# Attention scores on the whole array: key tiles with high and low parts in two halves of the rows

## The chip, the cores and the metric

The kernel runs on one core of one Trainium2 chip. The core has a matrix engine (TensorE, PE in the profile; PEld is its weight load), a vector engine (VectorE, DVE), an activation engine (ScalarE, ACT), a general engine (GpSimd, POOL) and an engine that only issues transfers (SyncE, SP). Each engine works through its own queue in order; semaphores tie the queues together. The on-chip memory has 128 partitions (rows); matrix results land in a separate memory, PSUM, in banks of 512 float32 per partition. The metric is the device time of one execution in microseconds (us); lower is better.

## The reference

Two layers act on a sequence of 1024 tokens of width 1024, in float32: first a gated linear recurrence, then sliding-window attention. Each is followed by a layer norm, a gated feed-forward part with a short convolution, and another layer norm. The change touches the attention alone:

```python
# 16 query heads, 4 key/value heads, head size 64, window 128; block j of 128 queries sees key blocks j-1 and j
q = (h @ w_q).reshape(B, nb, 128, 4, 4, 64)
logits = einsum('bntgrd,bnsgd->bngrts', q, keys_of_blocks_j_minus_1_and_j) * 64 ** -0.5
logits = where(mask, logits + bias, -inf)
m = maximum(logits.max(-1), sink)
p = exp(logits - m[..., None])
o = einsum('bngrts,bnsgd->bntgrd', p, values) / (p.sum(-1) + exp(sink - m))
mix = o.reshape(B, S, D) @ w_out
```

Keys and values are projected once, from the output of the first layer.

## The kernel before

**Float32 products.** TensorE multiplies in a rounded format (`F32R`). So most operands are kept as a high part (the rounded value, made by a ScalarE copy) and a low part (the value less its high part, made by a VectorE subtraction in `low_part`), and a product is three matmuls: high by high, high by low, low by high. These are lines L169 to L171 in `mm3`, with 512 or 256 columns. Plain float32 matmuls are L175 (`mm32`), transposes L179 (`tr`). `split`, `split_into` and `unit` make the two parts of a loaded weight in the buffer `HL` (ScalarE L151, VectorE L144) or of activations in `T`, the transposed input of all projections (ScalarE L196, VectorE L144).

**Start of the attention stage (L1097 to L1316).** While the second layer norm of layer 1 still finishes its last four token blocks (`ln_mid`: VectorE L232, transposes L179, ScalarE L244 and VectorE L246 out of one PSUM tile, then the split into `T`), `k_part` projects keys, `v_part` values, each for a part of the tokens. `k_part` gets, per half of 512 tokens and per pair `c` of key heads, one PSUM tile `ps` with head e = 0 in partitions 0 to 63 and head e = 1 in 64 to 127 (`es` is a head's own half of the partitions, `os` the other one). ScalarE writes the high part of each head into both halves of the partitions of `Kh` (L1133, L1134), VectorE the low part into `Kl` (L1136).

**Queries.** There are eight column groups c = 0..7, each one query head of two key groups (e = 0, 1; 128 columns). `q_proj` projects group c + 1 in two halves of 512 tokens while group c is attended. `q_split` then makes, out of the PSUM tile, the high part in the head's own partitions (ScalarE L1186, two instructions of 64x512) and the low part in the other partitions of the same tile `q` (VectorE L1188, two instructions).

**Scores.** `attend(c, bp, q)` is a generator that takes two blocks of 128 queries (bp = 0..3) through seven stages, with a `yield` after each: (1) scores on TensorE (L1200: queries' high and low rows by `Kh`, the whole array; L1203: the high rows of one head by `Kl`, half the rows) and ScalarE's copy of the scores of the block itself into `X` (L1205); (2) VectorE puts the scores of the block before over the masked places (L1209), GpSimd adds the bias (L1212, L1215); (3) VectorE takes the maximum (L1220, L1223), ScalarE the exponentials and their sums (L1227, L1229); (4) VectorE normalises (L1231 to L1233); (5) TensorE transposes (L179); (6) VectorE masks out of PSUM into `W` (L1241); (7) TensorE multiplies by the values (L175), ScalarE copies the result into `Y` (L1254) or, for c = 7, splits it into `T`.

**Order.** The loop from L1319 writes the order of TensorE, ScalarE, VectorE and GpSimd out by hand: what an engine gets in this loop it runs in just this order. A step (c, bp) runs stage 1 of its own blocks, stage 7 of the blocks three steps back, stage 3 of those one step back, stage 2 of its own, stages 5 and 6 of those two steps back, a quarter of the next group's projection (12 matmuls of `mm3`), stage 4 of those one step back, then `q_split` of a half that is done (at bp = 2 for half 0 and at bp = 0 of the next group for half 1), then the low parts that wait in the list `lows`. At bp = 0 of c < 6 ScalarE then casts the query weights of group c + 2 (L151); from c = 5, bp = 1 on, at the end of four steps, it casts parts of the output weights, and `Y_to_T` casts attention results into `T`. In the second step `v_part(3)` is put in between. Semaphores are placed by the framework from the reads and writes of each tile, not by hand.

PSUM tiles: `psmm` (one bank, four buffers) for projections, transposes and value products, `psax` (two banks, two buffers) for the scores.

Of the kernel before, what the change touches and what calls it, by code (L numbers as in the profile page):

```python
# [10 lines left out]
F32 = mybir.dt.float32  # L11
F32R = mybir.dt.float32r
U8 = mybir.dt.uint8
AF = mybir.ActivationFunctionType
ALU = mybir.AluOpType

P = 128
S = 1024
# [69 lines left out]
def trunk(ctx: ExitStack, tc: tile.TileContext, a: dict, out: bass.AP):  # L88
    nc = tc.nc
# [25 lines left out]
    def psmm():  # L115
        return mmp.tile([P, 512], F32, name="psmm")

    def psax():
        return axp.tile([P, 1024], F32, name="psax")
# [9 lines left out]
    def raw_tail(pool):  # L129
        tail["raw"] = [pool.tile([P, 1024], F32, name=f"raw{i}") for i in range(3)]  # L130
# [37 lines left out]
    def mm3(ps, st, mv, start, stop, n=512):  # L168
        nc.tensor.matmul(ps, st(0), mv(0), start=start, stop=False)  # L169
        nc.tensor.matmul(ps, st(0), mv(1), start=False, stop=False)  # L170
        nc.tensor.matmul(ps, st(1), mv(0), start=False, stop=stop)  # L171
        od.t += 3 * n / 2365.0
# [9 lines left out]
    def proj_T(hl, half, ps):  # L182
        for kc in range(KC):
            mm3(ps, lambda i: hl[:, i, kc, :], lambda i: T[:, i, kc, half * 512:(half + 1) * 512],
                kc == 0, kc == KC - 1)
            od.tick()
# [476 lines left out]
    with tc.tile_pool(name="t", bufs=1, reuse_waits="tile") as raws, hgrn_pool as hp:  # L663
# [40 lines left out]
        with tc.tile_pool(name="ep", bufs=1, reuse_waits="tile") as ep:  # L704
# [50 lines left out]
            ps = psmm()  # L755
# [212 lines left out]
        for i in range(2 * pairs):  # L968
            for s in range(8 * NH):
                for r in free:  # L970
                    at = next(n for n in range(s + 2, 9 * NH) if n not in busy and n not in sums)
# [99 lines left out]
        ps = psax()  # L1071
# [25 lines left out]
    with (tc.tile_pool(name="ta", bufs=1, reuse_waits="tile") as raws,  # L1097
          tc.tile_pool(name="at", bufs=1, reuse_waits="tile") as at):
        raw_tail(raws)
        Kh = at.tile([P, 2, 2, S], F32R, name="Kh")  # L1100
        tri = at.tile([P, 2, P], F32, name="tri")
        nc.scalar.dma_start(tri, a["tri"])
        sk = at.tile([P, 16], F32, name="sk")
# [7 lines left out]
                                                       ap=[[0, P], [1, 512]]))  # L1111
        wkv = a["shared_w_kv"]
        wkvv = wkv.rearrange("(kc p) c -> p kc c", p=P)
        Kl = at.tile([P, 2, S], F32R, name="Kl")
        Vt = at.tile([P, NB, 256], F32, name="Vt")
        khl, uv = [], []
        for c in range(2):
# [8 lines left out]
        def k_part(half):  # L1126
            ts = slice(half * 512, (half + 1) * 512)
            for c in range(2):
                ps = psmm()
                proj_T(khl[c], half, ps)  # L1130
                heads = [(slice(64 * e, 64 * e + 64), slice(64 - 64 * e, 128 - 64 * e)) for e in range(2)]
                for e, (es, os) in enumerate(heads):
                    nc.scalar.copy(Kh[es, c, e, ts], ps[es])  # L1133
                    nc.scalar.copy(Kh[os, c, e, ts], ps[es])  # L1134
                for e, (es, os) in enumerate(heads):
                    nc.vector.tensor_tensor(Kl[es, c, ts], ps[es], Kh[es, c, e, ts].bitcast(F32), op=ALU.subtract)  # L1136
        nsk = at.tile([P, 16], F32, name="nsk")
        nc.gpsimd.tensor_scalar(nsk, sk, -1.0, None, op0=ALU.mult)

# [27 lines left out]
        def q_proj(hl):  # L1167
            qs, done = [], []
            yield qs, done
            for half in range(2):  # L1170
                q = at.tile([P, 2, 512], F32R, name="q", bufs=3)
                qs.append(q)
                ps = psmm()
                for kc in range(KC):
                    mm3(ps, lambda i: hl[:, i, kc, :], lambda i: T[:, i, kc, half * 512:(half + 1) * 512],
                        kc == 0, kc == KC - 1)
                    od.tick()
                    if kc % 2 == 1 and kc < KC - 1:
                        yield
                done.append((q, ps))  # L1180
                yield

        def q_split(q, ps):
            heads = [(slice(64 * e, 64 * e + 64), slice(64 - 64 * e, 128 - 64 * e)) for e in range(2)]
            for e, (es, os) in enumerate(heads):
                nc.scalar.activation(q[es, e, :], ps[es], AF.Copy, scale=0.125)  # L1186
            for e, (es, os) in enumerate(heads):
                nc.vector.scalar_tensor_tensor(q[os, e, :], ps[es], 0.125, q[es, e, :].bitcast(F32),  # L1188
                                               op0=ALU.mult, op1=ALU.subtract)

        def attend(c, bp, q):
            pp, r = divmod(c, 4)
            ps = psax()
            pv = ps.rearrange("p (e j s) -> p e j s", e=2, j=2)
            for jj in range(2):
                j = 2 * bp + jj
                lo = P if j == 0 else 0
                qs, ks = slice((j % 4) * P, (j % 4 + 1) * P), slice((j - 1) * P + lo, (j + 1) * P)
                for e in range(2):
                    nc.tensor.matmul(pv[:, e, jj, lo:], q[bp // 2][:, e, qs], Kh[:, pp, e, ks], start=True, stop=False)  # L1200
                for e in range(2):
                    es = slice(64 * e, 64 * e + 64)
                    nc.tensor.matmul(pv[:, e, jj, lo:], q[bp // 2][es, e, qs], Kl[es, pp, ks], start=False, stop=True)  # L1203
            X = at.tile([P, 2, 2, P], F32, name="X", bufs=4)
            nc.scalar.copy(X, pv[:, :, :, P:])  # L1205
            yield
# [48 lines left out]
            else:  # L1255
                ts = slice(bp * 256, (bp + 1) * 256)
# [36 lines left out]
        with tc.manual_schedule(engines={EN.PE, EN.Activation, EN.DVE, EN.Pool}):  # L1293
            od.finish(lns[:4])
            late = [od.spawn(ln_rows(range(1), rows, 2.5, h2d), 6.0)]
            k_part(0)
            for tp in range(3):
                od.finish(lns[2 * tp:2 * tp + 2])
# [4 lines left out]
            hl = q_unit(0)  # L1303
            make_lows()
            k_part(1)
            g = q_proj(hl)
            q, done = next(g)
            hl = q_unit(1)
# [10 lines left out]
            for c in range(8):  # L1319
                fill = q_proj(hl) if c < 7 else last_filler()  # L1320
                nq, nd = next(fill)
                for bp in range(4):
                    it = attend(c, bp, q)
                    prev = [None] * (3 - len(flight)) + flight
                    if 4 * c + bp in moves:
                        Y_to_T(*moves[4 * c + bp], lows)
                    stage(it)
                    stage(prev[0])
                    stage(prev[2])
                    stage(it)  # L1330
                    stage(prev[1])
                    stage(prev[1])
                    stage(fill)
                    stage(prev[2])
                    while done:
                        q_split(*done.pop(0))
                    make_lows()
                    if bp == 0 and c < 6:
                        hl = q_unit(c + 2)
                    stage(fill)  # L1340
                    if len(flight) > 2:
                        flight.pop(0)
                    done.extend(nd)
                    nd.clear()
                    if c == 0 and bp == 1:
                        v_part(3)
                    if 0 <= 4 * c + bp - 21 < 4:
                        ring["hl"] = 4 * c + bp - 21
                        us.extend(out_unit(rows2, 4 * c + bp - 21, lows))
                    flight.append(it)  # L1350
                q = nq
            a29, a30, a31 = flight
            for _ in range(2):
                ps = psax()
# [55 lines left out]
```

## Time and profile before

| what | value |
|---|---|
| median of three runs | 2218.3 us (2216.71 to 2218.33) |
| span of the profiled execution, first to last instruction | 2212.6 us |
| TensorE busy | 2177.4 us (98%) |
| VectorE busy | 1787.0 us (81%) |
| ScalarE busy | 931.6 us (42%) |
| GpSimd busy | 177.7 us (8%) |
| steps of the attention loop | from 1291.7 to about 1476 us of the span |

The profiled execution's own time is its span; the rest up to the median of the runs lies before its first and behind its last instruction. Times in the rows count from the span's start. A row of the view in order of time has start, length, engine, line, operation, output <- inputs, shape, and how many equal instructions in a row it merges; in square brackets stands the idle time before it and what ended that. The ends of matmuls are modelled, so the distance between two starts tells more than a length. A row of waits has the waiting instruction, what it waited for, the total time, how often and the longest. A row of groups has the count, total busy time, mean time of one in ns, and the idle time before.

### The profile page before, as it was taken

Reading aid. Unit: us, or ns where it says so; the run is one execution under the profiler, and the core shown is the slowest. Engines: PE = TensorE matmul, PEld = TensorE weight load, DVE = VectorE, ACT = ScalarE, POOL = GpSimd, SP = SyncE. Lnnn points to the kernel's source line nnn. Section 1 sums busy time; section 2 is a strip of 40 time slices with the busy share of each in tenths; the row PEclk is TensorE's granted clock in tenths of the full one; section 3 lists DMA queues with packets and bytes.
Section 4 is the critical chain, followed back from the end, with each engine's and each line's share of the span. In section 5 each row is a group of like instructions: output and inputs, shape, how many; then the busy total and the mean of one; then the engine's idle time right before and its main releaser. Section 6 shows DMA issues by size and latency. Waiting matters only on the chain.

```text
span 2212.6 us, 33398 instructions
## 1 busy us (share of the span) xinstructions
PE 2177.4 (98%) x13135; PEld 1812.6 (82%) x13135; DVE 1787.0 (81%) x2415; ACT 931.6 (42%) x1601; POOL 177.7 (8%) x196
## 2 busy tenths in 40 slices
PE   8999999999999999999999999999999999999998
PEld 7888888888888888887888887778888888887887
DVE  2777666566789888888997788887899888889987
ACT  4333333332844443344334446655554443343431
POOL 0121111210100000000000012211000000000001
PEclk9999999999999999999999999999999999999999
DMA  5555443252222222238854431114123222249663
GB/s 196 191 191 172 153 172 116 69 125 86 87 85 86 84 78 86 86 96 272 279 171 130 115 89 34 34 63 138 67 96 96 78 75 85 86 144 318 202 215 134
DMA packets 231943, 281.16 MB, mean 127 GB/s; under 512 B 29977, under 2 KB 160746, under 8 KB 228970
## 3 DMA queue, kind: packets, MB, share of 16 engines
q1 hardware_dynamic: 228736, 276.53, 38.5%
q10 hardware_dynamic: 3050, 2.49, 0.9%
q8 instruction: 103, 1.69, 0.3%
q14 instruction: 54, 0.44, 0.1%
HBM read 213.96 MB, written 65.01 MB: 126 GB/s over the span
## 4 chain that ended last, share of the span: by engine, by line
PE 82%; DVE 9%; DMA 3%; ACT 3%; issue 2%; POOL 1%; SPq 0%; ACTq 0%; DVEq 0%; POOLq 0%
PE psmm L169 17%; PE psmm L171 16%; PE psmm L170 16%; PE psax L171 8%; PE psax L169 8%; PE psax L170 8%; PE psax L175 3%; DVE T L144 1%; PE psmm L175 1%; DMA rx<-in_ffn_w_in_dram 1%; DVE HL L144 1%; PE psax L179 1%; ACT Y L244 1%; PE psax L1200 1%; PE psax L1203 1%
## 5 line engine op out<-in xcount | busy, mean ns | idle before, releaser
L169 PE MATMUL psmm<-T,HL 128*128 128x512 f32 x768 | 308.1, 401 | 0.0
L170 PE MATMUL psmm<-T,HL 128*128 128x512 f32 x768 | 300.7, 392 | 3.8 <-DVE T L144 2.1
L171 PE MATMUL psmm<-T,HL 128*128 128x512 f32 x768 | 301.3, 392 | 0.0
L474 DVE SCALAR_TENSOR_TENSOR Y<-Y,cwt 128x1023 f32<-128x1023 f32 (+1 forms) x176 | 225.3, 1280 | 40.1 <-ACT Y L472 39.9
L472 ACT ACTIVATE Y<-Y,cwt 128x1024 f32<-128x1024 f32 x88 | 109.1, 1240 | 263.6 <-DVE Y L461 260.0
L169 PE MATMUL psmm<-HL,T 128*128 128x256 f32 (+1 forms) x656 | 199.6, 304 | 1.5 <-ACT T L196 1.5
L171 PE MATMUL psmm<-HL,T 128*128 128x256 f32 (+1 forms) x656 | 195.4, 298 | 1.6 <-DVE T L144 1.6
L170 PE MATMUL psmm<-HL,T 128*128 128x256 f32 (+1 forms) x656 | 195.1, 297 | 1.2 <-DVE HL L144 1.2
L196 ACT CAST HL<-rx 128x1024 fp32r<-128x1024 f32 (+1 forms) x137 | 140.3, 1045 | 122.6 <-DMA rx<-in_ffn_w_in_dram 33.3
L144 DVE TENSOR_TENSOR HL<-rx,HL 128x1024 fp32r<-128x1024 f32 (+1 forms) x137 | 165.9, 1213 | 14.9 <-ACT HL L196 14.3
L171 PEld LDWEIGHTS psmm<-T,HL 128*128 128x128 f32 x768 | 144.6, 188 | 33.5 <-issue 1.9
L170 PEld LDWEIGHTS psmm<-T,HL 128*128 128x128 f32 x768 | 144.7, 188 | 31.3 <-DVE T L144 2.9
L169 PEld LDWEIGHTS psmm<-T,HL 128*128 128x128 f32 x768 | 144.6, 188 | 31.3 <-issue 1.4
L171 PE MATMUL psax<-T,HL 128*128 128x512 f32 x352 | 137.6, 391 | 0.0
L169 PE MATMUL psax<-T,HL 128*128 128x512 f32 x352 | 137.5, 391 | 0.0
L170 PE MATMUL psax<-T,HL 128*128 128x512 f32 x352 | 137.4, 390 | 0.0
L169 PEld LDWEIGHTS psmm<-HL,T 128*128 128x128 f32 x656 | 126.2, 192 | 8.1 <-issue 2.5
L171 PEld LDWEIGHTS psmm<-HL,T 128*128 128x128 f32 x656 | 126.0, 192 | 5.7 <-DVE T L144 2.5
L170 PEld LDWEIGHTS psmm<-HL,T 128*128 128x128 f32 x656 | 126.2, 192 | 4.9 <-DVE HL L144 1.7
L218 POOL TENSOR_TENSOR rs<-rs,nhalf 128x1 f32<-128x1 f32 x32 | 26.0, 813 | 1291.4 <-DVE rs L217 1291.1
L853 POOL TENSOR_TENSOR kp<-kp,tot 128x512 f32<-128x512 f32 x48 | 72.9, 1519 | 290.0 <-PE psax L175 149.3
L144 DVE TENSOR_TENSOR HL<-raw,HL 128x1024 fp32r<-128x1024 f32 x51 | 64.0, 1254 | 21.7 <-ACT HL L151 21.6
(295 smaller groups left out, 5257.9 us busy)
## 6 DMA issues: line engine op xcount, KB each, us to landing
rx<-in_ffn_w_in_dram SPq DMA_DIRECT2D x136, 256.0 KB, 3.4
rx<-gd SPq DMA_DIRECT2D x118, 256.0 KB, 3.7
Y<-in_ffn_w_out_dram SPq DMA_DIRECT2D x44, 512.0 KB, 6.0
bsd<-Y SPq DMA_DIRECT2D x22, 1024.0 KB, 4.8
gd<-Y SPq DMA_DIRECT2D x44, 512.0 KB, 2.7
rx<-in_ffn_w_out_dram SPq DMA_DIRECT2D x54, 256.0 KB, 4.0
R<-bsd SPq DMA_DIRECT2D x44, 256.0 KB, 4.3
Y<-in_ffn_w_in_dram SPq DMA_DIRECT2D x40, 256.0 KB, 3.3
```

The lines of the kernel that those rows point to most:

```text
L144: make = lambda e: e.tensor_tensor(lo, src, hi.bitcast(F32), op=ALU.subtract)
L169: nc.tensor.matmul(ps, st(0), mv(0), start=start, stop=False)
L170: nc.tensor.matmul(ps, st(0), mv(1), start=False, stop=False)
L171: nc.tensor.matmul(ps, st(1), mv(0), start=False, stop=stop)
L175: nc.tensor.matmul(ps, lhsT, rhs, start=start, stop=stop, **kw)
L179: nc.tensor.transpose(ps, src, ident)
L196: nc.scalar.copy(hi, src)
L218: nc.gpsimd.tensor_tensor(rs, rs, nhalf, op=ALU.pow)
L244: nc.scalar.activation(hf[:, kc, :], ps[:, k * P:(k + 1) * P], AF.Identity, bias=shift, scale=scale)
L472: nc.scalar.activation(c, u, AF.Identity, bias=cwt[:, l, 3, ci:ci + 1], scale=cwt[:, l, 2, ci:ci + 1])
L474: nc.vector.scalar_tensor_tensor(c[:, sh:], u[:, :S - sh], cwt[:, l, 2 - sh, ci:ci + 1], c[:, sh:], op0=ALU.mult, op1=ALU.add)
L853: (nc.gpsimd if i else nc.vector).tensor_tensor(kv[:, :, 0, :], kv[:, :, 0, :], tv[:, :, 1:2].to_broadcast([P, nb, m]), op=ALU.mult)
```

## The change

The key tile `K` holds, for each head, the high part in the head's own half of the partitions and the low part in the other half; `Kl` is gone. The high part of the queries is written into both halves of the partitions: so one whole-array matmul gives high by high plus high by low. The low part of the queries goes into a tile of its own, `QB[half]`, in the head's own partitions; its other partitions are set to zero once, by four GpSimd memsets. A second whole-array matmul, `QB` by `K`, adds low by high. There are eight matmuls in a step as before, now all of 128 rows, and the two of one head follow each other.

In `k_part` ScalarE writes two copies per tile in place of four. In `q_split` it writes four in place of two: the two new ones read the same PSUM tile and stand behind the two VectorE low parts in program order.

```diff
-        Kh = at.tile([P, 2, 2, S], F32R, name="Kh")
+        K = at.tile([P, 2, 2, S], F32R, name="K")
+        QB = [at.tile([P, 2, 512], F32R, name=f"QB{i}") for i in range(2)]
+        for t in QB:
+            for e in range(2):
+                nc.gpsimd.memset(t[64 - 64 * e:128 - 64 * e, e, :].bitcast(F32), 0.0)
...
-        Kl = at.tile([P, 2, S], F32R, name="Kl")
...
                 for e, (es, os) in enumerate(heads):
-                    nc.scalar.copy(Kh[es, c, e, ts], ps[es])
-                    nc.scalar.copy(Kh[os, c, e, ts], ps[es])
+                    nc.scalar.copy(K[es, c, e, ts], ps[es])
                 for e, (es, os) in enumerate(heads):
-                    nc.vector.tensor_tensor(Kl[es, c, ts], ps[es], Kh[es, c, e, ts].bitcast(F32), op=ALU.subtract)
+                    nc.vector.tensor_tensor(K[os, c, e, ts], ps[es], K[es, c, e, ts].bitcast(F32), op=ALU.subtract)
...
-                q = at.tile([P, 2, 512], F32R, name="q", bufs=3)
+                q = at.tile([P, 2, 512], F32R, name="q", bufs=3), QB[half]
...
+            qh, ql = q
             for e, (es, os) in enumerate(heads):
-                nc.scalar.activation(q[es, e, :], ps[es], AF.Copy, scale=0.125)
+                nc.scalar.activation(qh[es, e, :], ps[es], AF.Copy, scale=0.125)
             for e, (es, os) in enumerate(heads):
-                nc.vector.scalar_tensor_tensor(q[os, e, :], ps[es], 0.125, q[es, e, :].bitcast(F32),
+                nc.vector.scalar_tensor_tensor(ql[es, e, :], ps[es], 0.125, qh[es, e, :].bitcast(F32),
                                                op0=ALU.mult, op1=ALU.subtract)
+            for e, (es, os) in enumerate(heads):
+                nc.scalar.activation(qh[os, e, :], ps[es], AF.Copy, scale=0.125)
...
                 for e in range(2):
-                    nc.tensor.matmul(pv[:, e, jj, lo:], q[bp // 2][:, e, qs], Kh[:, pp, e, ks], start=True, stop=False)
-                for e in range(2):
-                    es = slice(64 * e, 64 * e + 64)
-                    nc.tensor.matmul(pv[:, e, jj, lo:], q[bp // 2][es, e, qs], Kl[es, pp, ks], start=False, stop=True)
+                    for part in range(2):
+                        nc.tensor.matmul(pv[:, e, jj, lo:], q[bp // 2][part][:, e, qs], K[:, pp, e, ks],
+                                         start=part == 0, stop=part == 1)
```

## The prediction

> **What bounds the kernel now.** I read the page's engine shares first, then the stretches of the attention stage (1292 to 1476 us), then instructions in order of time on TensorE, ScalarE and VectorE, last the waits and the chain that ended last. Below are the span, then three stretches: the fifth, seventh and eighth column groups (c = 4, 6, 7). After the colon: length, then busy time of PE, PEld, DVE, ACT, POOL, then clock and DMA.
>
> ```profile
> span 2212.6 us, 33398 instructions
> ```
> ```profile
> 1383.93:1406.56 22.63, 22.63 (x158) 17.84 (x157) 19.16 (x43) 13.66 (x49) 6.58 (x10) 1.00 0.10 30
> 1429.18:1451.81 22.63, 22.63 (x158) 17.84 (x156) 21.57 (x45) 15.68 (x47) 4.80 (x7) 1.00 0.04 13
> 1451.81:1476.18 24.37, 22.91 (x168) 17.49 (x166) 22.87 (x53) 14.12 (x55) 8.09 (x7) 1.00 0.00 1
> ```
>
> TensorE paces c = 4 (22.63 busy of 22.63, full clock) and so, by the same length, the groups before it. In c = 6 VectorE is within about 1 us of full. The chain that ended last (start, length, what) says where the lead changes:
>
> ```profile
> 1425.12 0.87 PE psmm L175 x12
> ...
> 1430.27 1.22 DVE HL L144
> ...
> 1460.75 1.24 DVE T L144
> 1462.03 0.50 PE psmm L171
> ```
>
> Up to 1425 the chain is on TensorE, from 1430 to 1462 on VectorE, and at 1462.03 TensorE goes on only after a low part from VectorE. So what TensorE gains before that counts only as far as VectorE's place in its queue moves too. In c = 4 VectorE loses this to waits (total, times, longest):
>
> ```profile
> DVE X L1209 <- ACT X L1205: 1.4, 2, 1.2
> ...
> DVE Y L1241 <- PE psmm L179: 0.8, 2, 0.5
> ```
>
> Both stand behind TensorE (the first through the ScalarE copy of the scores), so 1.4 + 0.8 = 2.2 us a group is what VectorE can win by a faster TensorE.
>
> **The change, part by part: TensorE.** One step of the scores, in order of time:
>
> ```profile
> 1355.78 0.40 PE L1200 MATMUL psax<-Kh,q 128*128 128x256 f32 x2
> 1356.10 0.39 PE L1203 MATMUL psax<-Kl,q 64*128 64x256 f32 x2
> 1356.42 0.50 PE L1200 MATMUL psax<-Kh,q 128*128 128x256 f32 x2
> 1356.85 0.39 PE L1203 MATMUL psax<-Kl,q 64*128 64x256 f32 x2
> 1357.17 0.93 PE L175 MATMUL psmm<-Y,Vt 128*64 128x128 f32 x12
> ```
>
> The eight matmuls take 1357.17 - 1355.78 = 1.39 us, with a change between whole array and half rows four times, the last one into L175. The new form has eight whole-array matmuls of the same width in a row. Their pace is that of the projections with 256 columns, of which six in a row read (first and last):
>
> ```profile
> 1300.11 0.28 PE L169 MATMUL psmm<-HL,T 128*128 128x256 f32 x1
> ...
> 1300.71 0.28 PE L171 MATMUL psmm<-HL,T 128*128 128x256 f32 x1
> ```
>
> That is 0.60 / 5 = 0.12 apart. Leaving the whole array costs 1356.10 - 1355.78 - 0.12 = 0.20 for the last of a pair. New block: 7 x 0.12 + 0.20 = 1.04, a saving of 0.35; in the first step of each group half the tiles are narrower, where I take 0.25 (an estimate). A group saves 3 x 0.35 + 0.25 = 1.3, so TensorE alone would need 21.3. All eight groups: 10.4.
>
> **ScalarE and VectorE in the split of the queries.** Per half and group ScalarE gets two more copies of 64x512 out of the same PSUM bank that the two VectorE low parts read, and they stand behind these in program order. What the trace shows of two engines that read one bank (ScalarE and VectorE, two places):
>
> ```profile
> 1214.92 0.81 ACT L244 ACTIVATE R<-psax,par 128x128 f32<-128x128 f32 x2 [0.83 <-DVE T L144]
> ```
> ```profile
> 1215.76 0.73 DVE L246 TENSOR_SCALAR R<-psax,par 128x128 f32<-128x128 f32 x2 [0.30 <-ACT R L244]
> ```
> ```profile
> 1275.59 0.58 ACT L1133 CAST Kh<-psmm 64x512 fp32r<-64x512 f32 x1 [3.93 <-PE psmm L171]
> ...
> 1277.37 0.58 ACT L1134 CAST Kh<-psmm 64x512 fp32r<-64x512 f32 x1
> ```
> ```profile
> 1277.99 1.39 DVE L1136 TENSOR_TENSOR Kl<-psmm,Kh 64x512 fp32r<-64x512 f32 x2 [2.41 <-ACT Kh L1134]
> ```
>
> L246 uses other columns than L244, in and out, and still waits to its end (1215.73). L1136's first half needs only the first of the four copies and waits for the fourth, which reads the other 64 partitions. So reads of one bank by two engines are kept in program order, by the whole bank. The trace has no ScalarE read behind a VectorE read; between "starts at once" and "waits for both low parts" I take the second, because these rows show that order for the mirrored case. In its section "PSUM bank collisions raise a hardware error", the Trainium skill's page "PSUM — Partial Sum Buffer" says that ScalarE and VectorE reading one bank on the same 32 partitions at once is an error, "ScalarE-read with VectorE-read included", and must be guarded by semaphores; by that the new copies wait too, and the sum is the one below.
>
> What that wait holds up, from the half-1 split of c = 4 and the step behind it (ScalarE, then VectorE):
>
> ```profile
> 1388.30 1.19 ACT L1186 ACTIVATE q<-psmm 64x512 fp32r<-64x512 f32 x2
> 1389.52 1.05 ACT L151 CAST HL<-raw 128x1024 fp32r<-128x1024 f32 x1
> 1391.05 0.59 ACT L1205 COPY X<-psax 128x512 f32<-128x512 f32 x1 [0.48 <-PE psax L1203]
> 1392.12 0.37 ACT L1254 COPY Y<-psmm 128x256 f32<-128x256 f32 x1 [0.49 <-PE psmm L175]
> 1392.39 0.41 ACT L1227 ACTIVATE X<-X,nm 128x128 f32<-128x128 f32 x1
> ...
> 1393.96 0.19 ACT L1229 ACTIVATE se<-se 128x4 f32<-128x4 f32 x1
> ```
> ```profile
> 1389.57 1.41 DVE L1188 SCALAR_TENSOR_TENSOR q<-psmm,q 64x512 fp32r<-64x512 f32 x2
> 1391.01 0.69 DVE L1220 TENSOR_REDUCE nm<-X 128x4 f32<-128x512 f32 x1
> ...
> 1391.92 0.78 DVE L1209 COPY_PREDICATED X<-msk,psax 128x256 f32<-128x256 uint8 x2
> 1392.71 1.29 DVE L1241 TENSOR_TENSOR W<-psmm,tri 128x512 f32<-128x512 f32 x2
> 1394.18 0.16 DVE L1231 TENSOR_TENSOR dn<-dn,se 128x4 f32<-128x4 f32 x1 [0.18 <-ACT se L1229]
> ...
> 1395.20 1.22 DVE L144 TENSOR_TENSOR HL<-raw,HL 128x1024 fp32r<-128x1024 f32 x1
> ```
>
> Today L1205 waits only for TensorE. After: the low parts end at 1389.57 + 1.41 = 1390.98; two copies (1.19, handover 0.05) to 1392.22; the cast L151 behind them (1.05) to 1393.27; the score copy L1205 (0.59) to 1393.86. L1209, which needs it, starts at 1393.89 in place of 1391.92. Behind L1205 come L1254 (0.37, to 1394.23) and the exponentials, 1392.39 to 1394.15 = 1.76, to 1395.99. L1231 waits for them: 1396.02 in place of 1394.18. VectorE loses 1.85.
>
> The half-0 split has no cast behind it: score copy to 1.83 after the low parts, L1209 at 1.86 in place of 0.94 (1391.92 - 1390.98), so 0.95 lost. Together 2.8 a group, and the 2.2 of waits on TensorE go: +0.6 a group. VectorE's own cycle becomes about 22.63 + 0.6 = 23.2, more than TensorE's 21.3, and paces the stage.
>
> Ledger of VectorE's place:
> - c = 0: 0. TensorE gains 1.3, but one loss of 0.95 comes at its end; the other falls beside the value projection, 48 matmuls of 0.12 in the second step.
> - c = 1 to 4: 4 x 0.6 = +2.4.
> - c = 5: out-projection casts follow the half-0 split too, but a low part like L144 (1395.20, 1.13 to the next instruction by the reduce's usual start) stands between on VectorE and covers as much: 0.85 there, 1.85 + 0.85 - 2.2 = +0.5.
> - c = 6: 2 x 0.85 = +1.7, with nothing left to win, since VectorE hardly waits (21.57 of 22.63).
> - c = 7: the last split ends at the low part before 1462.03; behind it VectorE has slack. TensorE's last block: -0.35.
>
> **Keys, zeros and memory.** The key part does two ScalarE copies in place of four; the low parts keep their size. Where it is on the path:
>
> ```profile
> 1248.65 1.39 DVE L1136 TENSOR_TENSOR Kl<-psmm,Kh 64x512 fp32r<-64x512 f32 x2 [0.99 <-ACT Kh L1134]
> ```
> ```profile
> 1250.94 0.63 PE L179 MATMUL psax<-ident,Y 128*128 128x128 f32 x4 [1.33 <-DVE q L246]
> ```
>
> The 0.99 of waiting before L1136 goes; the transposes at 1250.94 then come up to 0.99 earlier, and the layer norm's own splits hand some of it back. Ends 0 and -0.99, taken -0.6. The four memsets on GpSimd are half as wide as this one, and stand ahead of an instruction that waits far longer:
>
> ```profile
> L700 POOL MEMSET A<- x1: 952/952/952, 1.4 to 1.4; 128x1024 f32 x1
> ```
> ```profile
> POOL nsk L1138 <- DMA X<-in_ln_ffn_b_dram: 24.1, 1, 24.1
> ```
>
> Below 4 x 0.95 = 3.8 inside 24.1: nothing. Without that cover the layer norm's `rs` behind them would pay up to 3.8. No DMA is moved, and the new tiles take the bytes of `Kl`. The PSUM tile of a split is freed 1.24 later; no TensorE wait names it today, taken as 0, at most 1.24 x 16 = 19.8.
>
> **Sum.** 2.4 + 0.5 + 1.7 - 0.35 - 0.6 = +3.65 on the profiled span of 2212.6. The runs' median is 2218.3, 5.7 above that span (what lies around it); the forecast keeps that distance: 2216.3 + 5.7 = 2222.
>
> **Rivals.**
> 1. The copies do not wait (faster). Then ScalarE has room (13.66 busy of 22.63, 2.4 more), VectorE moves with TensorE up to c = 4, 5 x 1.3 = 6.5, and nothing more until 1462.03; two blocks behind it 0.7, keys 0.6: -7.8, 2210.5. For it: no row shows ScalarE held in this order. Against: the two places above. It decides as soon as the copies start before the low parts end.
> 2. Each copy waits only for the low part of its own 64 partitions. Its end comes 0.6 sooner; the losses are 1.25 and 0.35, less than 2.2: c = 1 to 4 4 x -0.6, c = 5 -0.7, c = 6 +0.5, then -0.95: -3.55, 2214.8. Against: L1136 waited for copies of the other partitions. The Trainium skill's same page and section says that a different quadrant of the same bank does not collide; by that this rival would be open to the kernel, and the row of L1136 disagrees.
> 3. The change doesn't speed TensorE, since eight matmuls into two banks keep gaps. VectorE's cycle of 23.2 is still the longer one; the loss in c = 0 stands bare (0.95) and the last block saves nothing (0.35): 2223.3. Against: the pace of 0.12 above, three matmuls a group into one bank.
> 4. The later release of the PSUM tile stalls TensorE on half of the splits: 2222 + 8 x 1.24 = 2232.
>
> **How the numbers follow.** Forecast 0.71, rival 1 0.13, rival 2 0.08, rival 3 0.04, rival 4 0.04. A difference under 0.2% (4.4 us, so up to 2222.7) is about what a measurement can't tell from none. The forecast's own range is 2218 to 2226 (the losses per split are good to 0.3, over 11 splits), split about evenly by 2222.7. Slower: 0.71 x 0.48 + 0.03 + 0.04 = 0.41; faster: 0.13 + a third of rival 2 and a little = 0.17; within: 0.42. The range takes in rival 1's time at the low end and stops short of rival 4: 2210 to 2228.
>
> **What would show it.** Right: the new copies (in `q_split`) start just after L1188's second low part ends; the score copy L1205 behind a split waits for nothing on TensorE; VectorE's longest new wait is L1209 for it; L1231 waits more for the exponentials; a group lasts about 23.2 from the second on; the score block is 1.04 on TensorE, and TensorE's transposes and value matmuls start to wait for VectorE. Wrong: the copies run straight behind the first two, or each behind its own low part; groups of 21.3 or 22.0; TensorE waiting for a `psmm` tile.

## The result and the profile after

The changed kernel takes 2216.5 us (median of 13 runs) against 2218.3 for the kernel before (13 runs): ratio 0.9995, 95% interval 0.9987 to 1.0002. No difference can be told. The forecast gave a difference under 0.2% its largest chance, but only by a hair (0.42 against 0.41 for slower). Its point, 2222, is 5.5 us too high, and its own range of 2218 to 2226 misses 2216.5; only the wide range, stretched for the rivals, takes it in. That no difference came out is therefore in part luck, and there is more to learn from the point.

Line numbers after the change: the score matmuls are L1206, the score copy L1209, the predicated copy L1213, the maximum L1224 and L1227, the exponentials L1231 and L1233, the denominator L1235, the weights' mask L1245. In `q_split` ScalarE's high parts are L1189, VectorE's low parts L1191, ScalarE's new copies L1194.

The span, and the stretches c = 4, c = 6 and the last blocks (columns as in the forecast):

```profile
span 2213.8 us, 33413 instructions
```
```profile
1380.66:1403.26 22.60, 21.98 (x157) 18.26 (x156) 18.88 (x42) 15.70 (x54) 6.47 (x10) 1.00 0.10 30
1425.90:1450.65 24.75, 22.29 (x157) 18.25 (x156) 22.61 (x46) 18.15 (x57) 6.01 (x8) 1.00 0.08 23
1450.65:1476.00 25.35, 22.32 (x172) 18.07 (x170) 23.83 (x55) 16.75 (x62) 7.83 (x7) 1.00 0.00 1
```

Group c = 4 lasts 22.60 us where it lasted 22.63. But it is no longer the same bound: TensorE was busy for all of it, and now has 0.6 us to spare by this row. One block of scores, in order of time on TensorE:

```profile
1386.89 0.28 PE L1206 MATMUL psax<-K,q 128*128 128x256 f32 x1
1387.01 0.28 PE L1206 MATMUL psax<-K,QB 128*128 128x256 f32 x1
...
1387.72 0.28 PE L1206 MATMUL psax<-K,QB 128*128 128x256 f32 x1
1387.93 0.54 PE L175 MATMUL psmm<-Y,Vt 128*64 128x128 f32 x5
```

1387.93 - 1386.89 = 1.04, with 0.12 from one matmul to the next: to the hundredth what the forecast had. So TensorE got its gain, and something else took it. The waits of the same stretch (total, times, longest) name it:

```profile
DVE X L1213 <- ACT X L1209: 3.9, 3, 1.9
ACT q L1194 <- DVE QB L1191: 3.1, 2, 1.5
```

ScalarE stands twice a group behind VectorE's low parts, for 1.5 us each time, and VectorE then stands behind ScalarE's score copy. (The 3.9 counts the wait of about 0.97 at both edges of the stretch; one group has 0.97 + 1.91.) The half-1 split of c = 4 and the step behind it, first ScalarE, then VectorE:

```profile
1388.78 1.21 ACT L1194 ACTIVATE q<-psmm 64x512 fp32r<-64x512 f32 x2 [1.53 <-DVE QB L1191]
1389.89 1.03 ACT L151 CAST HL<-raw 128x1024 fp32r<-128x1024 f32 x1
1390.95 0.59 ACT L1209 COPY X<-psax 128x512 f32<-128x512 f32 x1
1391.43 0.38 ACT L1258 COPY Y<-psmm 128x256 f32<-128x256 f32 x1
1391.69 0.42 ACT L1231 ACTIVATE X<-X,nm 128x128 f32<-128x128 f32 x1
...
1393.25 0.20 ACT L1233 ACTIVATE se<-se 128x4 f32<-128x4 f32 x1
```
```profile
1387.34 1.40 DVE L1191 SCALAR_TENSOR_TENSOR QB<-psmm,q 64x512 fp32r<-64x512 f32 x2
...
1391.57 0.78 DVE L1213 COPY_PREDICATED X<-msk,psax 128x256 f32<-128x256 uint8 x2 [1.91 <-ACT X L1209]
1392.24 1.28 DVE L1245 TENSOR_TENSOR W<-psmm,tri 128x512 f32<-128x512 f32 x2
1393.48 0.33 DVE L1235 TENSOR_TENSOR dn<-dn,se 128x4 f32<-128x4 f32 x1
```

The first L1194 reads the 64 partitions that the first low part read. It starts at 1388.78, 0.04 behind the end (1387.34 + 1.40 = 1388.74) of the second low part, which reads the other 64. So the order holds for the bank as a whole, as the forecast took it. The chain that ended last, which the forecast had on TensorE up to 1425, runs here through both engines (start, length, what):

```profile
1388.05 0.70 DVE QB L1191
...
1389.39 0.33 ACT q L1194
...
1389.89 1.03 ACT HL L151
...
1390.95 0.60 ACT X L1209
```

### The profile page after: what moved, and what is told of

Its sections match the earlier page's. It is cut to its first block, busy times and chain, and to the rows that moved or that the text cites. A ratio compares the mean times of both kernels' runs of the same rounds, so it can differ in the third digit from the quotient of the medians.

```text
span 2213.8 us, 33413 instructions
## 1 busy us (share of the span) xinstructions
PE 2170.0 (98%) x13135; PEld 1814.7 (82%) x13135; DVE 1785.6 (81%) x2415; ACT 942.0 (43%) x1625; POOL 178.3 (8%) x200
## 4 chain that ended last, share of the span: by engine, by line
PE 73%; DVE 14%; ACT 5%; DMA 4%; issue 3%; POOL 1%; SPq 0%; ACTq 0%; DVEq 0%; POOLq 0%
PE psmm L169 15%; PE psmm L171 15%; PE psmm L170 15%; PE psax L171 7%; PE psax L169 7%; PE psax L170 7%; PE psax L175 3%; DVE T L144 2%; DVE HL L144 1%; DMA rx<-in_ffn_w_in_dram 1%; PE psax L179 1%; DVE Y L474 1%; ACT Y L244 1%; ACT T L196 1%; DVE QB L1191 1%
## 5 line engine op out<-in xcount | busy, mean ns | idle before, releaser
L196 ACT CAST HT<-rx 128x1024 fp32r<-128x1024 f32 (+1 forms) x51 | 43.8, 860 | 89.6 <-PE psmm L170 30.6
```

The source lines that it names most:

```text
L196: nc.scalar.copy(hi, src)
```

## The experiments

Single executions differ by up to 5.7 us in the time ahead of the first score (it starts between 1291.03 and 1296.75), and no edit goes with that: two kernels with the same key part, the changed one and e3, are its two ends. So the table has beside the medians the stage itself: from the first matmul of the scores to the first of the last block (in the changed kernel 1469.94 - 1291.03). Each ratio is to runs of the kernel before that were taken together with that kernel's.

| kernel | stage, us | groups c = 2 to 4 | c = 6 | c = 7, three steps | median, us | ratio to before, 95% interval |
|---|---|---|---|---|---|---|
| before | 178.46 | 22.63 | 22.63 | 18.37 | 2218.3 | |
| changed | 178.91 | 22.62 | 24.75 | 19.29 | 2216.5 | 0.9995 (0.9987 to 1.0002) |
| e1, copies from SBUF | 169.64 | 21.28 | 22.08 | 18.78 | 2207.4 | 0.9949 (0.9936 to 0.9963) |
| e2, copies first | 180.22 | 22.17 | 25.57 | 20.96 | 2221.4 | 1.0017 (1.0008 to 1.0026) |
| e3, copies on GpSimd | 170.21 | 21.28 | 22.60 | 18.83 | 2210.2 | 0.9957 (0.9943 to 0.9971) |
| e4, four key copies | 178.86 | 22.61 | 24.72 | 19.31 | 2219.2 (one run) | |
| e5, before with two changes | 173.31 | 21.85 | 22.01 | 19.01 | 2213.2 | 0.9974 (0.9964 to 0.9984) |
| e6, SBUF in half 0 | 173.26 | 21.70 | 24.03 | 18.76 | 2214.3 | 0.9979 (0.9969 to 0.9989) |
| e7, SBUF in half 1 | 171.11 | 21.28 | 22.98 | 19.29 | 2210.3 | 0.9964 (0.9952 to 0.9975) |
| e8, low parts on GpSimd | 174.42 | 21.28 | 26.75 | 18.44 | 2213.4 | 0.9979 (0.9970 to 0.9989) |
| e9, division on ScalarE | 173.58 | 21.28 | 22.40 | 22.40 | 2212.2 | 0.9977 (0.9968 to 0.9986) |

The theory after the result: what TensorE saved was lost to ScalarE's place behind VectorE on the PSUM bank of the queries. Its rival: ScalarE's two further copies cost that much by themselves, wherever they read.

**e1: the second copies read SBUF.** Against the changed kernel:

```diff
             for e, (es, os) in enumerate(heads):
-                nc.scalar.activation(qh[os, e, :], ps[es], AF.Copy, scale=0.125)
+                nc.scalar.copy(qh[os, e, :], qh[es, e, :].bitcast(F32))
```

> The second copies of the query high parts read the first copies in SBUF in place of the PSUM bank, so nothing on VectorE stands between them and the first ones. Theory (what the saved TensorE time lost was the order on the PSUM bank: ScalarE held behind VectorE's low parts, 3.1 us on two waits a group at the copies, then 3.9 a group on VectorE at the predicated copy of the scores): both waits shrink to what TensorE leaves (under 1.5 a group together), groups c = 1 to 4 fall from 22.6 to about 21.3, from c = 5 on VectorE keeps its own length, and the time is about 2210 (2208 to 2212), 6 to 8 us under the changed kernel. Rival (ScalarE's added work itself, 2.4 us a group standing ahead of the score copy, costs what TensorE saves, whoever waits): groups stay at 22.3 or more and the time is within 2 us of the changed kernel.

Measured: 2207.4 us, 0.5% under the kernel before. A group, its split on ScalarE, and the waits in it:

```profile
1378.29:1399.57 21.28, 21.28 (x157) 17.97 (x156) 19.08 (x42) 16.02 (x53) 6.60 (x10) 1.00 0.12 32
```
```profile
1383.52 1.25 ACT L1194 CAST q<-q 64x512 fp32r<-64x512 f32 x2
1384.79 1.05 ACT L151 CAST HL<-raw 128x1024 fp32r<-128x1024 f32 x1
1385.86 0.59 ACT L1209 COPY X<-psax 128x512 f32<-128x512 f32 x1
```
```profile
DVE X L1213 <- ACT X L1209: 0.9, 2, 0.5
DVE Y L1245 <- PE psmm L179: 0.5, 1, 0.5
```

The copies are as long as those out of PSUM (1.25 and 1.21 the pair), and ScalarE is as busy (16.02 and 15.70), but L1194 now has no wait, and TensorE is busy for all 21.28 us again. The rival falls. The whole difference to the changed kernel, 9.3 us of the stage, is the hold. The time is a little under the theory's 2208, because the theory left the groups from c = 5 on as they were. Against the changed kernel c = 5 falls by 1.36 (22.64 to 21.28), c = 6 by 2.67 and c = 7 by 0.51.

**e2: all copies out of PSUM first, low parts behind them.**

```diff
             for e, (es, os) in enumerate(heads):
                 nc.scalar.activation(qh[es, e, :], ps[es], AF.Copy, scale=0.125)
             for e, (es, os) in enumerate(heads):
+                nc.scalar.activation(qh[os, e, :], ps[es], AF.Copy, scale=0.125)
+            for e, (es, os) in enumerate(heads):
                 nc.vector.scalar_tensor_tensor(ql[es, e, :], ...)
-            for e, (es, os) in enumerate(heads):
-                nc.scalar.activation(qh[os, e, :], ps[es], AF.Copy, scale=0.125)
```

> All four ScalarE copies out of PSUM come first, the two low parts of VectorE behind them. Theory (reads of one bank by two engines go in program order, by the whole bank): VectorE's first low part of each split waits for the fourth copy, 1.2 us later than in the changed kernel, and ScalarE is held nowhere in the split; the hold moves from ScalarE to VectorE. The low part follows the copies, so the score copy on ScalarE is free about 1.4 us earlier per split; of the 3.9 us a group of waits at the predicated copy 2.8 go, and 2 x 1.2 = 2.4 come at the low parts if VectorE stands there already. Groups 22.0 to 22.6, time 2213 to 2217. Rival (each engine is ordered only by the 64 rows that it reads, so the low parts would not wait for the copies of the other rows): the low parts wait no longer than in the changed kernel, groups about 21.3, time about 2210, as with the copies taken from SBUF.

Measured in one group:

```profile
DVE QB L1193 <- ACT q L1191: 2.2, 2, 1.1
```

The first low part, which needs only the first copy, waits 1.1 us for the fourth: the same order by the bank, with VectorE as the one who waits. The rival, order by 64 rows, falls. The groups (22.17) are in the theory's range, but the time of 2221.4 is not. In c = 6 and c = 7, where VectorE is full, each wait of VectorE is paid whole: 25.57 and 20.96 against 24.75 and 19.29. That makes the stage 1.3 us longer than the changed kernel's. The rest of the 4.8 us between the medians lies outside the stage: in the profiled executions, 1.6 us ahead of the first score (1292.60 against 1291.03) and 2.7 us behind the first matmul of the last block. Its cause was not settled.

**e3: the second copies on GpSimd, out of SBUF.** Against the changed kernel:

```diff
+            for e, (es, os) in enumerate(heads):
+                nc.gpsimd.tensor_copy(qh[os, e, :], qh[es, e, :].bitcast(F32))
             for e, (es, os) in enumerate(heads):
                 nc.vector.scalar_tensor_tensor(ql[es, e, :], ...)
-            for e, (es, os) in enumerate(heads):
-                nc.scalar.activation(qh[os, e, :], ps[es], AF.Copy, scale=0.125)
```

> The second copies are made by GpSimd out of SBUF, so ScalarE has no more work than in the kernel before the change. Theory (the loss is ScalarE's hold behind VectorE): as with ScalarE's copies from SBUF, provided that GpSimd's copies (estimated at 1 to 2 us each, from its other instructions of 64x512) end before the scores of the next group ask for the queries: groups c = 1 to 4 about 21.3, time 2208 to 2212. If ScalarE's own 2.4 us a group were part of the loss, this run would lie 2 us or more under the one with ScalarE's copies from SBUF. If GpSimd's copies come late, TensorE waits at the first scores of a group for the queries, and the groups stay near 22.6.

```profile
L1191 POOL CAST q<-q 64x512 fp32r<-64x512 f32 x4 | 3.2, 803 | 1.9 <-ACT q L1189 1.8
```

Four copies of 0.80 us in a group, groups of 21.28, stage 170.21. With ScalarE's added work gone as well, the stage is not shorter than e1's but 0.6 us longer. So ScalarE's 2.4 us a group cost nothing by themselves that shows in the time. The 0.6 us are c = 6 (22.60 against 22.08); why it is longer was not looked into.

**e4: four key copies again.** Against the changed kernel:

```diff
                 for e, (es, os) in enumerate(heads):
                     nc.scalar.copy(K[es, c, e, ts], ps[es])
+                    nc.scalar.copy(K[os, c, e, ts], ps[es])
```

> The changed kernel with the two ScalarE copies a key tile put back that the change took out (they write the high part where the low part then goes, so the result is the same). Theory: the first score starts at 1291.7 as before the change, in place of 1291.0, and VectorE's low parts of the keys wait about 1 us longer for ScalarE. Rival (the 0.7 us at the first score come from elsewhere, such as differences between executions): the first score stays at 1291.0. The time is within 2 us of the changed kernel by either.

The first key copy and the first score matmul, in the changed kernel and then in e4:

```profile
1240.70 1.18 ACT L1136 CAST K<-psmm 64x512 fp32r<-64x512 f32 x2 [4.80 <-PE psmm L171]
...
1291.03 0.22 PE L1206 MATMUL psax<-K,q 128*128 128x128 f32 x1
```
```profile
1244.77 0.58 ACT L1136 CAST K<-psmm 64x512 fp32r<-64x512 f32 x1 [4.80 <-PE psmm L171]
...
1295.68 0.22 PE L1207 MATMUL psax<-K,q 128*128 128x128 f32 x1
```

The first score itself, at 1295.68, fits neither number that was expected: this execution ran 4 us late before the keys began. Measured from the first key copy it is 50.33 us in the changed kernel, 50.91 in e4, and 50.90 before the change (1291.72 - 1240.82). The other runs repeat it: all eight kernels with two copies a tile have 50.33 or 50.34, all three with four have 50.9. So the two copies that the change leaves out of each tile are worth 0.57 us at the first score.

**e5: the kernel before, with fewer changes between all rows and half.** Against the kernel before; the second pair of queries takes its low parts first:

```diff
-                for e in range(2):
-                    nc.tensor.matmul(..., q[bp // 2][:, e, qs], Kh[:, pp, e, ks], start=True, stop=False)
-                for e in range(2):
-                    es = slice(64 * e, 64 * e + 64)
-                    nc.tensor.matmul(..., q[bp // 2][es, e, qs], Kl[es, pp, ks], start=False, stop=True)
+                for part in ((0, 1), (1, 0))[jj]:
+                    for e in range(2):
+                        es = slice(64 * e, 64 * e + 64)
+                        if part == 0:
+                            nc.tensor.matmul(..., q[bp // 2][:, e, qs], Kh[:, pp, e, ks], start=jj == 0, stop=jj == 1)
+                        else:
+                            nc.tensor.matmul(..., q[bp // 2][es, e, qs], Kl[es, pp, ks], start=jj == 1, stop=jj == 0)
```

> The kernel before the change, with all its tiles and matmuls; only the second pair of queries takes its low parts ahead of its high parts, so that the array changes between all rows and half the rows two times inside a block of scores in place of three. Theory (the 0.35 us that a block saved is the price of those changes, about 0.20 each, and nothing in the data or the tiles): the block falls from 1.39 to about 1.20 us, groups c = 1 to 5 from 22.63 to about 21.9 (3 x 0.19 + 0.14), VectorE follows since nothing was added to it or to ScalarE, time about 2214 (2212 to 2216). Rival (a matmul on half the rows is itself slow): the block stays at 1.39 and the time within 1.5 us of 2218.

```profile
1386.08 0.40 PE L1203 MATMUL psax<-Kh,q 128*128 128x256 f32 x2
1386.40 0.51 PE L1206 MATMUL psax<-Kl,q 64*128 64x256 f32 x4
1386.84 0.50 PE L1203 MATMUL psax<-Kh,q 128*128 128x256 f32 x2
1387.28 0.45 PE L175 MATMUL psmm<-Y,Vt 128*64 128x128 f32 x4
```

1387.28 - 1386.08 = 1.20, the groups 21.85, the time 2213.2: all as the theory had it, and the rival falls. The half-row matmuls are not slow: four of them, with the change back to all rows, take 0.44 us (1386.84 - 1386.40), 0.11 each. But the theory's price of 0.20 for one change does not fit the three blocks. Before the change a block goes to half the rows twice (the second time it leaves them for L175) and takes 1.39; in e5 it goes there once and takes 1.20; in the changed kernel it never does and takes 1.04. So going to half the rows and back costs 0.16 to 0.19, some 0.09 a change. The 0.20 was the distance from the last whole-array matmul to the first half-row one, and 0.12 of it passes between any two matmuls of this width. This order of the same matmuls, with no new tile and no new copy, gains more than the change did.

**e6 and e7: one split with SBUF copies, the other with PSUM copies.** In both, `q_split` is told its half; e7 has `half == 1`:

```diff
-                nc.scalar.activation(qh[os, e, :], ps[es], AF.Copy, scale=0.125)
+                if half == 0:
+                    nc.scalar.copy(qh[os, e, :], qh[es, e, :].bitcast(F32))
+                else:
+                    nc.scalar.activation(qh[os, e, :], ps[es], AF.Copy, scale=0.125)
```

> The changed kernel; the second copies read SBUF in the half-0 splits, and PSUM, behind VectorE's low parts, in the half-1 splits as in the changed kernel. Theory (each PSUM-ordered split has its own price on VectorE, in the trace of the changed kernel 1.54 us for half 1 and 0.81 for half 0, and TensorE needs 21.28): groups c = 1 to 4 are VectorE's 22.61 less 0.81 less 0.17 (what the half-0 split gains with SBUF copies) = 21.6 to 21.8; time 2210 to 2213. Rival (the group is set by one loop through both engines, in which one split alone matters): 21.3 or 22.6.

> The mirror: SBUF copies in the half-1 splits, PSUM copies in the half-0 splits. Theory: 22.61 less 1.54 and plus the 0.15 that the half-1 split keeps losing with SBUF copies is 21.2, so TensorE's 21.28 sets the group (21.3 to 21.4); time 2207 to 2210, little over that with SBUF copies in both. Rival (one split alone matters): as for the other run, with the other sign.

A group of e6, then of e7:

```profile
1381.08:1402.79 21.71, 21.47 (x157) 18.10 (x156) 18.94 (x42) 15.90 (x55) 6.51 (x11) 1.00 0.12 31
```
```profile
1377.88:1399.16 21.28, 21.28 (x157) 17.97 (x156) 19.02 (x42) 15.96 (x54) 6.59 (x11) 1.00 0.11 32
```

21.7 and 21.28, as expected from the two prices. (The expectation of e6 took the denominator's start as its mark. By the mark used further down the half-0 split costs 0.91, with nothing to gain beyond it: 22.60 - 0.91 = 21.69.) So each held split has a price of its own on VectorE, the prices add, and a group is the longer of VectorE's sum and TensorE's 21.28. With the half-1 split freed TensorE is the bound again, and the half-0 hold is hidden, up to c = 5. In c = 6, where VectorE is full, it is paid again (22.98 against e1's 22.08). Both medians lie a little over what was expected, e6's by 1.3 us and e7's by 0.3.

**e8: SBUF copies, and low parts of the late groups on GpSimd.** Against e1:

```diff
+        elif isinstance(eng, tuple):
+            eng[0].append(lambda: make(nc.gpsimd))
...
-                        Y_to_T(*moves[4 * c + bp], lows)
+                        Y_to_T(*moves[4 * c + bp], (lows,) if 4 * c + bp < 28 else lows)
...
-                        us.extend(out_unit(rows2, 4 * c + bp - 21, lows))
+                        us.extend(out_unit(rows2, 4 * c + bp - 21, (lows,)))
```

> SBUF copies in both halves, and of VectorE's low parts in the last groups six (four of the out-projection weights, two of the attention output, 128x1024, 1.15 us each on VectorE) are made by GpSimd, whose bias adds leave it 2.8 to 5.5 us free a step. Theory (with the hold gone, TensorE's gain is lost only from c = 6 on, 0.8 us in group c = 6, 2.6 in the three steps of c = 7, because VectorE is full there): 1 to 3 us of these 3.4 go, time 2204 to 2206.5. Rival (GpSimd takes about 2.6 us for one, twice its 1.3 for 128x512, ahead of the next bias add, or slows VectorE beside it): the bias adds come late, VectorE waits for them, and the time is 2207 or more.

The rival's side, by 6 us against e1 and by a way that it had only in half a sentence. GpSimd first, then VectorE:

```profile
1417.34 2.40 POOL L144 TENSOR_TENSOR HL<-raw,HL 128x1024 fp32r<-128x1024 f32 x1
...
1424.72 2.37 POOL L144 TENSOR_TENSOR HL<-raw,HL 128x1024 fp32r<-128x1024 f32 x1
```
```profile
1417.64 2.63 DVE L1239 TENSOR_TENSOR X<-X,dn 128x512 f32<-128x512 f32 x1
...
1423.22 1.28 DVE L1247 TENSOR_TENSOR W<-psmm,tri 128x512 f32<-128x512 f32 x2
...
1425.05 2.59 DVE L1239 TENSOR_TENSOR X<-X,dn 128x512 f32<-128x512 f32 x1
```

VectorE's division of 128x512 takes 2.6 us in place of 0.69 (L1237 in e1), and ends 0.5 us behind GpSimd's subtraction: 1417.64 + 2.63 = 1420.27 against 1417.34 + 2.40 = 1419.74, and 1427.64 against 1427.09. That is less than its own 0.69, so it did most of its work only when GpSimd was done. All six divisions beside such a subtraction take 2.59 to 2.63. VectorE saves 1.15 us by a low part that it gives away and loses 1.9 by the division. The group c = 6 grows from e1's 22.08 to 26.75.

**e9: SBUF copies, and the division of c = 6 and 7 on ScalarE.** Against e1:

```diff
-            nc.vector.tensor_tensor(X, X, dn.unsqueeze(3).to_broadcast([P, 2, 2, P]), op=ALU.mult)
+            if c < 6:
+                nc.vector.tensor_tensor(X, X, dn.unsqueeze(3).to_broadcast([P, 2, 2, P]), op=ALU.mult)
+            else:
+                for i in range(4):
+                    nc.scalar.activation(X[:, i // 2, i % 2, :], X[:, i // 2, i % 2, :], AF.Copy,
+                                         scale=dn[:, i // 2, i % 2:i % 2 + 1])
```

> SBUF copies in both halves, low parts on VectorE again; in groups c = 6 and 7 the division of the scores by their sum (on VectorE 0.61 us a step, 4.9 us in eight steps) is done by ScalarE, four 128x128 pieces of about 0.29 to 0.4 us, 1.2 to 1.6 us a step. This asks again what the run with low parts on GpSimd asked, without a second engine beside VectorE's division. Theory (what TensorE's gain still loses from c = 6 on, 0.8 + 2.6 us, is lost because VectorE is full there): most of the 3.4 us go, the stage from the first score to the last block lasts 166.5 to 168.5 us in place of 169.6, time 2204 to 2206.5. Rival (ScalarE, 4.9 to 5.1 us busy in a step of 6.7 there, becomes the full engine, or its wait for VectorE's reciprocal holds the score copies behind it): the stage lasts 169.6 or more, the time is 2207 or more.

The rival again. From 1415 to 1468:

```profile
DVE QB L1191 <- ACT q L1189: 5.0, 2, 2.5
ACT X L1241 <- DVE dn L1236: 4.6, 6, 0.9
...
DVE X L1213 <- ACT X L1209: 3.1, 4, 1.4
```

ScalarE stands behind VectorE's reciprocal (L1236), and VectorE behind ScalarE's late copies. VectorE's work fell, and its waits took the place, mostly in c = 7 (22.40 against e1's 18.78). So what e1 still loses behind c = 5, some 3 us, remains open: two tries to unload VectorE each put a new hold in.

## Why the prediction was right or wrong, point by point

**TensorE's block: right in size.** 1.04 for 1.39, and TensorE needs 21.28 a group where 21.3 was forecast (e1). One thing was left out: in c = 0 the projection stands right behind the scores in the first three steps, so the way back from half rows to the whole array fell there too, and c = 0 became 1.95 us shorter on TensorE (24.33 to 22.38), not 1.3.

**The order on the bank: right.** The copies start 0.04 us behind the second low part (rival 1 and rival 2 wrong, for this kernel), no wait of TensorE in the stage names a line of `q_split` (rival 4 wrong), and rival 3 was wrong by the block. The Trainium skill's "PSUM — Partial Sum Buffer", section "PSUM bank collisions raise a hardware error", has both rules that the forecast weighed: reads of one bank on the same 32 partitions need a guard, which the row of L1194 agrees with; and another quadrant of the bank is free, of which this kernel made no use. The row of L1136, which the forecast set against that second rule, shows the order that the framework put into the program, not what the chip would allow. No run here shows what the chip would do without the guard.

**The price of the hold, and what VectorE wins back: the mechanism right, both sizes off.** This is the step of the sum that failed: "Together 2.8 a group, and the 2.2 of waits on TensorE go: +0.6 a group." From the end of the low parts to the reciprocal, which stands right behind the denominator, the traces have (half 1 and then half 0, both in c = 4):

| | before (L1232) | changed (L1236) | loss | forecast |
|---|---|---|---|---|
| half-1 split | 3.40 (1394.38 - 1390.98) | 5.10 (1393.84 - 1388.74) | 1.70 | 1.85 |
| half-0 split | 3.23 (1405.69 - 1402.46) | 4.14 (1405.24 - 1401.10) | 0.91 | 0.95 |

```profile
1394.38 0.18 DVE L1232 RECIPROCAL dn<-dn 128x4 f32<-128x4 f32 x1
```
```profile
1393.84 0.18 DVE L1236 RECIPROCAL dn<-dn 128x4 f32<-128x4 f32 x1
```

(The denominator itself is a poor mark: where it waits for nothing it starts before L1245 ends and then lasts 0.33, where it had lasted 0.16. By its start the losses would read 1.54 and 0.81, but the instructions behind it are 1.70 and 0.91 late.)

The predicated copy came out to the tenth: 2.83 behind the low parts where 2.91 was forecast, and 1.89 where 1.86. Behind it ScalarE was quicker than forecast. The forecast laid ScalarE's instructions end to end with their full lengths. In the rows above, the attention copy starts at 1391.43 while the score copy runs to 1391.54, and the exponentials at 1391.69: 0.74 us behind the score copy's start, not 0.96. So the exponentials end at 1393.45, before VectorE is through L1245 (1393.52), and no longer set its place. Losses are 2.6 a group and not 2.8.

The larger miss is what VectorE won back: 22.63 + 2.61 - 22.60 = 2.64, not 2.2. The four waits that the forecast added up lasted 0.20, 0.26, 1.16 and 0.53 in the rows, 2.15 together. But an instruction that need not wait also starts about 0.1 before the one ahead of it ends, so their going brought 0.29, 0.37, 1.25 and 0.63, 2.5 together; the remaining 0.1 is small gains and losses elsewhere in the group. The longest of them, before and after:

```profile
1408.56 0.50 DVE L1209 COPY_PREDICATED X<-msk,psax 128x128 f32<-128x128 uint8 x2 [1.16 <-ACT X L1205]
```
```profile
1406.85 0.49 DVE L1213 COPY_PREDICATED X<-msk,psax 128x128 f32<-128x128 uint8 x2
```

The one ahead of it (L1223, L1227 after) starts at 1407.23 and at 1406.77 and lasts 0.16: the distance fell from 1.33 to 0.08. So +0.6 became 0.0, and the +2.4 of c = 1 to 4 with it. That a group of the changed kernel has just the old length is a coincidence of 2.6 lost and 2.6 won, not a common bound.

**The ledger, group by group.** VectorE's first maximum of a group, counted from the first score, is a good clock for its queue. In c = 1, 5 and 7, before and then after:

```profile
1323.12 0.69 DVE L1220 TENSOR_REDUCE nm<-X 128x4 f32<-128x512 f32 x1
...
1413.64 0.69 DVE L1220 TENSOR_REDUCE nm<-X 128x4 f32<-128x512 f32 x1
...
1461.89 0.68 DVE L1220 TENSOR_REDUCE nm<-X 128x4 f32<-128x512 f32 x1
```
```profile
1320.91 0.69 DVE L1224 TENSOR_REDUCE nm<-X 128x4 f32<-128x512 f32 x1
...
1411.40 0.69 DVE L1224 TENSOR_REDUCE nm<-X 128x4 f32<-128x512 f32 x1
...
1462.03 0.68 DVE L1224 TENSOR_REDUCE nm<-X 128x4 f32<-128x512 f32 x1
```

Less 1291.72 and 1291.03: the changed kernel is 1.52 early at c = 1 (29.88 against 31.40), 1.55 early at c = 5 (120.37 against 121.92), and 0.83 late at c = 7 (171.00 against 170.17). So c = 0 brought -1.52, where the ledger had 0: TensorE came 1.95 earlier to the end of the group, and VectorE followed for most of it. The half-0 hold in this group did cost 0.94 (VectorE was 1.51 early at the end of the low parts and 0.57 at the next maximum), but waits behind it gave as much back. c = 1 to 4 brought 0.0, where the ledger had +2.4. c = 5 and 6 brought +2.38, where it had 0.5 + 1.7 = 2.2: right in the sum, but by luck. The group c = 5, from its first maximum to that of c = 6, grew by 1.48 and not by 0.5, since only 0.9 of the 2.2 was there to be won: the wait of 1.16 and the 0.53 behind it do not stand in this group, where the out-projection's low parts keep VectorE busy. And c = 6 grew by 0.90 and not by 1.7, since its two holds, with a low part behind them, lost 0.53 each where 0.85 was taken (the one of this kind in c = 5 lost 0.71). The two wrong entries that do not cancel, c = 0 and c = 1 to 4, are 3.9 us together.

**Keys: right.** -0.6 forecast, -0.57 measured (first key copy to first score, repeated in every run). **Memsets, tile release, DMA: nothing**, as taken: the first score comes no later, and no transfer is named among the waits above.

**Sum.** To the first matmul of the last block the ledger had 0 + 2.4 + 0.5 + 1.7 = +4.6; the trace has 178.91 - 178.46 = +0.45. That is 4.1 of the 5.5 us by which the point was high. The rest lies within what single executions differ by: the profiled spans have +1.2, the medians -1.8. Rival 1, at 2210.5 us, is what e1 made of the change; it stood 3 us too high, of which 2 are these: c = 0 gained 1.95 in place of 1.3, and c = 5, which it left out, 1.35 (22.63 to 21.28).

## What to carry to other kernels

Before a new reader is put on a PSUM bank that another engine reads, look for the same values in SBUF: the copy is as long there, and the order on the bank goes (here 9.3 us of the stage). Price such a hold at each place where it stands and by what stands behind it in the queue; the prices add until the next engine is the bound. And look first at the order of the matmuls: putting equal shapes side by side gave 5 us with no new work.

## What the runs showed of the hardware that was not expected

- Work on GpSimd can stop VectorE: with a 128x1024 subtraction of two SBUF tiles on GpSimd (2.4 us), VectorE's multiplication of two SBUF tiles took 2.6 us in place of 0.69 (e8). L1247, which has one input in PSUM and one in SBUF, kept the 1.28 of its pair beside GpSimd's bias add (1423.22 against 1423.47 to 1424.78). The Trainium skill's "SBUF — State Buffer", section "Who interferes with whom", says that a VectorE instruction with two SBUF inputs contends with a GpSimd instruction that reads SBUF, and that the ports they share are "an exclusive lock"; the trace agrees, with the division, which started 0.30 us later, ending 0.53 behind the subtraction.
- Instructions that follow each other without a wait often overlap by about 0.1 us, on ScalarE (1391.43 against 1390.95 + 0.59 = 1391.54) and on VectorE (1406.85 against 1406.77 + 0.16 = 1406.93). So the full lengths, added up, can be more than a chain of them takes, and a wait that goes can be worth 0.1 us more than its length.
- Taking a block's matmuls to half the rows and back costs 0.16 to 0.19 us: the block of scores takes 1.39 us with two such visits, 1.20 with one (e5) and 1.04 with none.
